# Attention over head pairs: narrow and wide query tiles by turns, alternating memory for queries and keys, and a second ring of score banks

## The chip, the cores and the metric

The kernel runs on one core of a Trainium2 chip. A core has a matrix engine (TensorE, PE in the profile, with its weight loads shown as PEld), a vector engine (VectorE, DVE), a scalar engine for activations (ScalarE, ACT), a general engine (GpSimd, POOL) and a queue engine that issues transfers (SyncE, SP). Each engine runs its own instructions in order, and semaphores order them against each other. Matmuls write into PSUM, here eight banks of 128 partitions by 512 fp32 values; other tiles lie in SBUF; the rest is in the device's main memory and is moved by DMA.

The metric is the device time of the whole kernel in microseconds (us), as the median of several executions. A profile shows one execution.

## The reference

One layer of a hybrid decoder on an input of 1024 positions by 1024 features: a joint projection, then an attention group and an RWKV-7 group of eight heads of 64 each, an output projection and a feed-forward block. What matters here is the attention group:

```
for (window, dilation) in ((128, 1), (512, 4), (2048, 16)):
    query t attends to t, t-d, t-2d, ..., t-window          (causal)
o = sum over the three branches of exp(m - m_all) * acc, divided by the same sum over l
attn = rms_norm(o) * attn_out_gain
mixed = concat([attn, rw]) @ w_out
```

The three branches have the same scores and differ only in which keys they admit. The kernel therefore computes one softmax per head over all causal keys, with a bias that depends on the distance of key and query only: minus infinity where no branch admits the key, and the logarithm of the number of branches otherwise. This bias is the tile `stripT`.

## The kernel before

The whole program is written as straight code through a layer that places tiles in rings of buffers (a pool's `tag` is a ring, `bufs` its length), sets the semaphores, and orders the instructions of ACT, DVE, POOL and SP by a plan of its own, with a priority that `hi_pri` raises. The order on PE is the one in which the code is traced, from line 1055 on by hand (`pe_order`). A tile's first write waits until the last reader of the tile that held its buffer before is done.

Attention handles four pairs of heads (`p`), per pair eight tiles of 128 queries (`i`) and two heads (`h`): 64 steps `m`. Tile `i` has 128 * (i + 1) causal keys, so tile 0 is the narrowest and tile 7 the widest. The parts of a step:

- `at_load(p)` (line 847) brings queries and keys of a pair from main memory through the ring `raw` (two buffers, shared with the values), splits them into a high and a low part on POOL and DVE (`qs`, `kh`, `kl`), and leaves six tiles of 4 KB per partition. The rings `qs`, `kh` and `kl` have two buffers, one per head, so a pair's tiles take the places of the pair before.
- `at_s` (880) computes one tile's scores `pS` on PE in one or two banks (first 512 keys, then the rest), adds the bias and takes the row minimum on DVE (`mn`), and takes the exponential with its sum on ACT. The result is in `Sx`, a ring of three. The banks are of ring w (two banks); the second half goes to ring z (two banks) in pair 1 and in part of pair 2 (line 892).
- `at_t` (900) transposes `Sx` on PE into banks a and c, and copies them to `PT` (ring of six): the first four blocks on ACT, the others on DVE.
- `at_vt` (870) transposes the pair's values, through the same banks a and c, to `Vt` (one buffer).
- `at_v(p, i0)` (914) multiplies two tiles' `PT` by `Vt` into `po`: tiles 0 to 3 in bank b, tiles 4 to 7 in bank y. After every second call it divides by the sums into `ao` (one buffer), stores `ao` to `a_d`, and squares it for the norm (`sqa`, `sq4`).

The main loop (1089) issues in each step the scores of the tile two steps ahead, the transposes of its own tile, and after some steps an `at_v`. Tiles come in the order 0, 1, ... 7, each with head 0 and head 1. `at_load(p + 1)` is traced in a pair's second step. Between the steps lie the last steps of the projection that feeds attention (`rest`, up to step 6), the loads and splits of the output matrix's eight slabs (`load_wo`), and the output projection of the RWKV half for two token tiles (`r_ahead`, 1059: transposes `mxtr` and 24 matmuls `pm` each, in both banks of ring z) from steps 45 and 53 on. A third `r_ahead` stands at the end.

`open_mix` (955), at step 31, gives up the memory of the projection's inputs and opens the pools `tcomb` (attention's half of the output matrix) and `mix` (what the output projection needs). After the loop the norm's factor `sa` is computed on DVE, `half_a` (980) loads and scales the attention output `ma`, transposes it (`mxta`) and the rest of the output projection follows.

Of the kernel before, what the change touches and what calls it, by code (L numbers as in the profile page):

```python
# [17 lines left out]
P = 128  # L18
S = 1024
# [21 lines left out]
def hybrid_kernel(tc, x, par, cst, strip, win, wup_lora, gup, gnwb, grow, wout, wup, wdown, out, dbg=None):  # L41
# [22 lines left out]
    with (  # L64
# [779 lines left out]

        at, sx, pts, pos = {}, {}, {}, {}

        def at_load(p):

            QS, KH, KL = [], [], []
            for h in range(2):  # L850
                qr = ap_.tile([P, S], F32, name=f"qr{p}_{h}", tag="raw")
                for d in range(2):
                    nc.sync.dma_start(qr[own[d]], zs_d[12 + p, h * 64:h * 64 + 64, :])
                qs = ap_.tile([P, S], F32R, name=f"qs{p}_{h}", tag="qs")
                G.tensor_scalar(qs, qr, -0.125, 0.0, op0=OP.mult, op1=OP.add)
                V.scalar_tensor_tensor(qs[64:128], qr[64:128], -0.125, qs[64:128].bitcast(F32), OP.mult, OP.subtract)
                QS.append(qs)
            for h in range(2):
                kr = ap_.tile([P, S], F32, name=f"kr{p}_{h}", tag="raw")
                for d in range(2):  # L860
                    nc.sync.dma_start(kr[own[d]], zs_d[16 + p, h * 64:h * 64 + 64, :])
# [18 lines left out]
        def at_s(p, i, h):  # L880

            QS, KH, KL = at[p]
            w = P * (i + 1)
            if i == 0 and h == 0:
                at[p, "den"] = sm.tile([P, 8, 2], F32, name=f"den{p}", tag="den")
                at[p, "rden"] = sm.tile([P, 8, 2], F32, name=f"rden{p}", tag="rden")
# [27 lines left out]
        def at_v(p, i0):  # L914

            Vt, qg = at[p, "v"], i0 // 4
            if i0 % 4 == 0:
                pos[p, qg] = ps.tile([P, 4, 2, 64], F32, name=f"po{p}_{qg}", tag="by"[qg], bufs=1)
            po = pos[p, qg]
            for i in (i0, i0 + 1):  # L920
                for h in range(2):
                    PT = pts.pop((p, i, h))
                    for j in range(i + 1):
                        mm_h(po[:, i % 4, h], PT[:, j], Vt[:, j, h * 64:h * 64 + 64], j == 0, j == i)
            if i0 % 4 == 0:
                return
            rden = at[p, "rden"][:, 4 * qg:4 * qg + 4]
# [27 lines left out]
        def open_mix():  # L955
# [37 lines left out]
        def mix_x1(t, pm, y=None):  # L993
# [5 lines left out]
            if y is None:  # L999
                y = mp.tile([P, D], F32, name=f"y{t}", tag="y")  # L1000
                src = pm
# [57 lines left out]
        def r_ahead(i, keep):  # L1059
# [11 lines left out]
            if keep:  # L1071
                pms[i] = pm
                return
            part[i] = M["mp"].tile([P, D], F32, name=f"y{ORD[i]}", tag="y")
            for n in range(2):
                A.activation(part[i][:, n * 512:n * 512 + 512], pm[n], AF.Copy)

        ahead = {i: r_ahead(i, i == 2) for i in range(3)}
        LEAD = 28
        for _ in range(LEAD):  # L1080
            next(rest, None)
        hi_pri = lambda: tc.high_priority(offset=PRI[3])
        step = lambda m: (m // 16, m % 16 // 2, m % 2)
        with hi_pri():
            at_load(0)
            at_s(*step(0))
            at_s(*step(1))
            at_vt(0)
        for m in range(64):
            p, i, h = step(m)  # L1090
            with hi_pri():
                if i == 7:
                    at_t(p, i, h)
                    if h == 0:
                        at_v(p, 4)
                    else:
                        if p < 3:
                            at_s(p + 1, 0, 0)
                            at_s(p + 1, 0, 1)
                            at_v(p, 6)  # L1100
                            at_vt(p + 1)
                else:
                    at_s(p, (m % 16 + 2) // 2, h)
                    at_t(p, i, h)
                    if h == 1 and i in (2, 4):
                        at_v(p, i - 2)
                    if h == 1 and i == 0 and p < 3:
                        at_load(p + 1)
# [5 lines left out]
            if m in (13, 21) or m in (29, 37):  # L1114
                k = {13: 4, 21: 5, 29: 6, 37: 7}[m]
                load_wo(k, w2p, "w2")
            if m == 31:
                open_mix()
            if m in (43, 45, 47, 49):
                load_wo((m - 43) // 2, M["tp"], "woA")  # L1120
            for i_, m0 in ((0, 45), (1, 53)):
                if m0 <= m < m0 + 9:
# [8 lines left out]
        for _ in ahead[2]:  # L1131
            pass
        tp, tp_ctx, mp, mix_ctx = M["tp"], M["tc"], M["mp"], M["mc"]
        gpM = mp.tile([P, D], F32, name="gpM", bufs=1)
# [118 lines left out]
        HT = {k: v[1:] for k, v in TS.items()}  # L1253
        mix_ctx.__exit__(None, None, None)
        if "x1" in dbg:
            nc.sync.dma_start(dbg["x1"], x_d)
# [260 lines left out]
```

## Time and profile before

| | |
|---|---|
| median of 3 runs | 1368.56 us (1368.4 to 1368.89) |
| profiled execution | 1369.49 us; its span, first to last instruction, 1367.7 us |
| mean granted TensorE clock | 0.986 |
| bytes moved by DMA | 231.09 MB, 169 GB/s over the span |
| first scores to last `po` matmul | 479.02 to 645.63 us |

Busy times of the engines in the page are sums over the span; an engine that is busy half of the time may still set the end in one stage and have nothing to do in another. Views used further on: the page itself; groups of waits (engine and line that waited, what it waited for, total us, times, longest); the timeline (start and duration in us, engine, line, operation, output and inputs, shapes, count, in brackets the idle time before it and what ended it); busy times by stretch (length, then busy time and count for PE, PEld, DVE, ACT and POOL, then granted clock, DMA share and GB/s); and the chain of work that ended last (start, duration, engine and tile, count).

### The profile page before, as it was taken

Reading aid. Unit: us, or ns where it says so; the run is one execution under the profiler, and the core shown is the slowest. Engines: PE = TensorE matmul, PEld = TensorE weight load, DVE = VectorE, ACT = ScalarE, POOL = GpSimd, SP = SyncE. Lnnn points to the kernel's source line nnn. Section 1 sums busy time; section 2 is a strip of 40 time slices with the busy share of each in tenths; the row PEclk is TensorE's granted clock in tenths of the full one; section 3 lists DMA queues with packets and bytes.
Section 4 is the critical chain, followed back from the end, with each engine's and each line's share of the span. In section 5 each row is a group of like instructions: output and inputs, shape, how many; then the busy total and the mean of one; then the engine's idle time right before and its main releaser. Section 6 shows DMA issues by size and latency. Waiting matters only on the chain.

```text
span 1367.7 us, 23518 instructions
## 1 busy us (share of the span) xinstructions
PE 1291.0 (94%) x9360; PEld 1063.5 (78%) x9360; DVE 914.4 (67%) x1647; ACT 626.3 (46%) x1026; POOL 45.9 (3%) x56
## 2 busy tenths in 40 slices
PE   6999999999999988789998999999999999999997
PEld 5777888788777867678787788888888888888875
DVE  7867757531678576555698986777666776445686
ACT  7652324233455376455556444444343444443442
POOL 0000000000000101010000000000000002000110
PEclk9999999999999999999999999999999999999999
DMA  6346747676584663321333344443456995346554
GB/s 253 114 169 162 193 107 195 184 203 211 169 248 147 200 211 91 86 70 40 123 123 133 137 169 170 153 145 135 161 200 211 327 349 182 92 128 210 187 204 165
DMA packets 161197, 231.09 MB, mean 169 GB/s; under 512 B 51680, under 2 KB 88800, under 8 KB 161088
## 3 DMA queue, kind: packets, MB, share of 16 engines
q1 hardware_dynamic: 153024, 208.62, 47.2%
q10 hardware_dynamic: 8064, 20.98, 4.5%
q8 instruction: 73, 1.20, 0.4%
q14 instruction: 36, 0.29, 0.1%
HBM read 156.66 MB, written 72.89 MB: 168 GB/s over the span
## 4 chain that ended last, share of the span: by engine, by line
PE 74%; DVE 13%; DMA 6%; ACT 4%; issue 2%; SPq 0%; POOL 0%; DVEq 0%; ACTq 0%; POOLq 0%
PE X L47 11%; PE dX L47 8%; PE Z L47 6%; PE pm L47 6%; PE dZ L47 5%; PE z_aq L47 3%; PE dY L47 3%; PE z_av L47 3%; PE po L47 3%; PE z_ak L47 3%; PE Y L47 3%; PE z_v L47 3%; PE z_k L47 3%; PE pT L908 2%; PE pS L47 2%
## 5 line engine op out<-in xcount | busy, mean ns | idle before, releaser
L47 PE MATMUL dX<-wow,wou 128*128 128x512 f32 x768 | 176.2, 390 | 2.3 <-DVE wow L1179 1.6
L47 PEld LDWEIGHTS dX<-wow,wou 128*128 128x128 f32 x768 | 143.8, 188 | 34.1 <-DVE wow L1179 3.4
L47 PE MATMUL dZ<-wow,wou 128*128 128x512 f32 x384 | 87.4, 389 | 0.0
L47 PEld LDWEIGHTS dZ<-wow,wou 128*128 128x128 f32 x384 | 72.1, 188 | 15.0
L1178 ACT ACTIVATE wow<-wd 128x1024 fp32r<-128x1024 f32 x40 | 42.3, 1060 | 88.9 <-PE dZ L47 29.8
L1179 DVE TENSOR_TENSOR wou<-ur,wou 128x1024 fp32r<-128x1024 f32 x56 | 72.0, 1287 | 8.4 <-ACT wou L1178 8.3
L1179 DVE TENSOR_TENSOR wow<-wd,wow 128x1024 fp32r<-128x1024 f32 x40 | 49.9, 1250 | 34.7 <-ACT wow L1178 34.1
L1178 ACT ACTIVATE wou<-ur 128x1024 fp32r<-128x1024 f32 x56 | 58.5, 1048 | 20.9 <-DMA ur<-u_d 13.4
L908 PE MATMUL pT<-cst,S 128*128 128x128 f32 x288 | 47.1, 290 | 18.4 <-DVE PT L912 12.2
L898 ACT ACTIVATE S<-S,mn 128x128 f32<-128x128 f32 (+7 forms) x64 | 49.4, 772 | 19.2 <-DVE mn L896 18.4
L908 PEld LDWEIGHTS pT<-cst,S 128*128 128x128 f32 x288 | 34.4, 146 | 28.7 <-issue 11.1
L1265 ACT ACTIVATE r<-u 128x512 f32<-128x512 f32 x48 | 30.0, 626 | 52.4 <-DVE u L1263 52.0
L896 DVE CUSTOM_DVE_ANT_0 S<-pS,stripT 128x512 f32<-128x512 f32 (+3 forms) x64 | 37.6, 590 | 23.5 <-PE pS L47 18.6
L47 PE MATMUL pm<-WO,mxr 128*128 128x512 f32 x192 | 49.4, 400 | 0.5 <-DVE mxr L972 0.5
L47 PE MATMUL z_aq<-hT,wh_aq 128*128 128x512 f32 x128 | 46.5, 417 | 3.5 <-DVE ev_v L202 3.5
L1179 DVE TENSOR_TENSOR wow<-TK,wow 128x1024 fp32r<-128x1024 f32 x16 | 20.8, 1301 | 38.9 <-ACT wow L1178 38.9
L47 PE MATMUL z_k<-hT,wh_k 128*128 128x512 f32 x128 | 44.9, 412 | 1.7 <-DVE z L233 1.4
L47 PE MATMUL Z<-HB,wo 128*128 128x512 f32 x192 | 46.1, 389 | 0.0
L47 PE MATMUL pm<-WO,mxa 128*128 128x512 f32 x192 | 45.8, 394 | 0.0
L47 PE MATMUL X<-HB,wo 128*128 128x512 f32 x180 | 43.6, 390 | 1.6 <-ACT HB L1034 1.6
L47 PE MATMUL z_av<-hT,wh_av 128*128 128x512 f32 x128 | 44.9, 405 | 0.0
L910 ACT ACTIVATE PT<-pT 128x512 f32<-128x512 f32 (+3 forms) x64 | 32.8, 512 | 26.0 <-PE pT L908 17.2
(388 smaller groups left out, 3097.0 us busy)
## 6 DMA issues: line engine op xcount, KB each, us to landing
ur<-u_d SPq DMA_DIRECT2D x56, 512.0 KB, 4.3
wd<-in_wdown_dram SPq DMA_DIRECT2D x40, 512.0 KB, 4.2
u_d<-S SPq DMA_DIRECT2D x64, 256.0 KB, 2.1
u_d<-u SPq DMA_DIRECT2D x48, 256.0 KB, 2.1
wr_upa<-in_wup_dram SPq DMA_DIRECT2D x16, 512.0 KB, 3.6
wr_upb<-in_wup_dram SPq DMA_DIRECT2D x16, 512.0 KB, 4.0
TK<-in_wdown_dram SPq DMA_DIRECT2D x16, 512.0 KB, 7.3
x<-in_x_dram SPq DMA_DIRECT2D x8, 512.0 KB, 8.1
```

What stands on the lines that cost most here:

```text
L47: return PE.matmul(o, lhsT, rhs, start=start, stop=stop, skip_group_check=True)
L896: V.tensor_tensor_reduce(Sx[:, lo:hi], pS[:, :hi - lo], stripT[:, so:so + hi - lo], 1.0, 3e38 if k == 0 else mn[:, 0:1], OP.add, OP.min, a ...
L898: A.activation(Sx[:, :w], Sx[:, :w], AF.Exp, scale=-1.0, bias=mn[:, nbk - 1:nbk], accum_out=at[p, "den"][:, i, h:h + 1])
L908: PE.transpose(pt[:, j], Sx[:, (4 * k + j) * P:(4 * k + j + 1) * P], ident)
L910: A.activation(PT[:, 0:nb_], pt[:, 0:nb_], AF.Copy)
L1178: A.activation(w[:, 0, 0:n], raw, AF.Copy)
L1179: E.tensor_tensor(w[:, 1, 0:n], raw, w[:, 0, 0:n].bitcast(F32), OP.subtract)
L1265: A.activation(r, src, AF.Relu)
```

## The change

- The tiles of a pair come in the order 0, 4, 1, 5, 2, 6, 3, 7 (`TO`).
- Queries and keys of pairs 1 and 3 go to a pool of their own, `attn1`, with the same six tiles; it lies in the memory that `open_mix` frees, and `open_mix` moves from step 31 to step 7, where pair 1's load is traced too. Pairs 2 and 3 are loaded from steps 17 and 33.
- The second half of a tile's scores uses ring z from pair 1 on, and in pair 0 for tiles 6 and 7.
- `at_v` opens both `po` banks at a pair's start and follows the order `TO`; both are closed by `at_out`, one behind the other, at the pair's end. The last `at_v` of a pair is issued in the second step of the next pair, and `at_vt` behind it.
- Slabs of the output matrix are loaded at other steps (`WOM`), the two `r_ahead` start at steps 38 and 48, the tile `y` gets a pool of its own (`mixy`), and the pool `mix` is opened after the loop, when `attn1` is closed.

```diff
-        at, sx, pts, pos = {}, {}, {}, {}
+        at, sx, pts, pos, aset = {}, {}, {}, {}, {0: ap_}
+        TO = [0,4,1,5,2,6,3,7]
...
-                qs = ap_.tile([P, S], F32R, name=f"qs{p}_{h}", tag="qs")
+                qs = aset[p % 2].tile([P, S], F32R, name=f"qs{p}_{h}", tag=f"qs{h}", bufs=1)
...
-                kh = ap_.tile([P, S], F32R, name=f"kh{p}_{h}", tag="kh")
-                kl = ap_.tile([P, S], F32R, name=f"kl{p}_{h}", tag="kl")
+                kh = aset[p % 2].tile([P, S], F32R, name=f"kh{p}_{h}", tag=f"kh{h}", bufs=1)
+                kl = aset[p % 2].tile([P, S], F32R, name=f"kl{p}_{h}", tag=f"kl{h}", bufs=1)
...
-                pS = ps.tile([P, 512], F32, name=f"pS{p}_{i}_{h}_{k}", tag="wz"[k] if p == 1 or p == 2 and i < 6 else "w")
+                pS = ps.tile([P, 512], F32, name=f"pS{p}_{i}_{h}_{k}", tag="wz"[k] if p > 0 or TO.index(i) > 4 else "w")
...
-            Vt, qg = at[p, "v"], i0 // 4
-            if i0 % 4 == 0:
-                pos[p, qg] = ps.tile([P, 4, 2, 64], F32, name=f"po{p}_{qg}", tag="by"[qg], bufs=1)
-            po = pos[p, qg]
-            for i in (i0, i0 + 1):
+            Vt = at[p, "v"]
+            if i0 == 0:
+                pos[p] = [ps.tile([P, 4, 2, 64], F32, name=f"po{p}_{qg}", tag="by"[qg], bufs=1) for qg in range(2)]
+            for i in TO[i0:i0 + 2]:
                 for h in range(2):
                     PT = pts.pop((p, i, h))
                     for j in range(i + 1):
-                        mm_h(po[:, i % 4, h], PT[:, j], Vt[:, j, h * 64:h * 64 + 64], j == 0, j == i)
-            if i0 % 4 == 0:
-                return
+                        mm_h(pos[p][i // 4][:, i % 4, h], PT[:, j], Vt[:, j, h * 64:h * 64 + 64], j == 0, j == i)
+                if i0 == 6:
+                    at_out(p, i // 4)
+
+        def at_out(p, qg):
+            po = pos[p][qg]
             rden = at[p, "rden"][:, 4 * qg:4 * qg + 4]
...
-            M["mc"] = tc.tile_pool(name="mix", bufs=2)
-            M["mp"] = M["mc"].__enter__()
+            M["yc"] = tc.tile_pool(name="mixy", bufs=2)
+            M["yp"] = M["yc"].__enter__()
+            M["ac"] = tc.tile_pool(name="attn1", bufs=1)
+            aset[1] = M["ac"].__enter__()
...
+        WOM = {17: 4, 19: 5, 33: 6, 35: 7, 37: 0, 49: 1, 51: 2, 53: 3}
...
-        step = lambda m: (m // 16, m % 16 // 2, m % 2)
+        step = lambda m: (m // 16, TO[m % 16 // 2], m % 2)
...
         for m in range(64):
-            p, i, h = step(m)
+            p, h = m // 16, m % 2
+            i = m % 16 // 2
             with hi_pri():
...
+                if m + 2 < 64:
+                    at_s(*step(m + 2))
+                at_t(*step(m))
+                if h == 1 and i % 2 == 0 and m > 1:
+                    at_v(*((p, i - 2) if i else (p - 1, 6)))
+                if h == 1 and i == 0:
+                    at_vt(p)
+                if m == 17 or m == 33:
+                    at_load(p + 1)
...
             if m == 7:
                 for _ in rest:
                     pass
...
+                open_mix()
+                with hi_pri():
+                    at_load(1)
...
-            for i_, m0 in ((0, 45), (1, 53)):
+            for i_, m0 in ((0, 38), (1, 48)):
...
+        M["ac"].__exit__(None, None, None)
+        tp, tp_ctx = M["tp"], M["tc"]
+        mix_ctx = tc.tile_pool(name="mix", bufs=2)
+        mp = M["mp"] = mix_ctx.__enter__()
```

More of the change, by code (lines that the diff above doesn't have):

```diff
@@ L883, in at_s @@
             w = P * (i + 1)
-            if i == 0 and h == 0:
+            if (p, "den") not in at:
                 at[p, "den"] = sm.tile([P, 8, 2], F32, name=f"den{p}", tag="den")
@@ L999, in mix_x1 @@
             if y is None:
-                y = mp.tile([P, D], F32, name=f"y{t}", tag="y")
+                y = M["yp"].tile([P, D], F32, name=f"y{t}", tag="y")
                 src = pm
@@ L1073, in r_ahead @@
                 return
-            part[i] = M["mp"].tile([P, D], F32, name=f"y{ORD[i]}", tag="y")
+            part[i] = M["yp"].tile([P, D], F32, name=f"y{ORD[i]}", tag="y")
             for n in range(2):
@@ L1113, in hybrid_kernel @@
                     pass
[L1114 to L1117, printed above, removed]
                 open_mix()
-            if m in (43, 45, 47, 49):
-                load_wo((m - 43) // 2, M["tp"], "woA")
-            for i_, m0 in ((0, 45), (1, 53)):
+                with hi_pri():
+                    at_load(1)
+            if m in WOM:
+                k = WOM[m]
+                load_wo(k, w2p if k > 3 else M["tp"], "w2" if k > 3 else "woA")
+            for i_, m0 in ((0, 38), (1, 48)):
                 if m0 <= m < m0 + 9:
@@ L1254, in hybrid_kernel @@
         mix_ctx.__exit__(None, None, None)
+        M["yc"].__exit__(None, None, None)
         if "x1" in dbg:
```

19 lines of the change are left out of this document (removed).

## The prediction

> **What bounds the kernel now.** First the page's totals and its chain that ended last.
>
> ```profile
> span 1367.7 us, 23518 instructions
> ...
> PE 1291.0 (94%) x9360; PEld 1063.5 (78%) x9360; DVE 914.4 (67%) x1647; ACT 626.3 (46%) x1026; POOL 45.9 (3%) x56
> ...
> PE 74%; DVE 13%; DMA 6%; ACT 4%; issue 2%; SPq 0%; POOL 0%; DVEq 0%; ACTq 0%; POOLq 0%
> ```
>
> TensorE (PE) bounds the kernel, so the change is worth what it takes out of PE's idle and slow time in the attention loop, the only stage whose work is reordered. The stage runs from the first scores (479.02 us) to the end of the last `po` matmuls (645.63), 166.6 us. I cut it where each head pair's first score matmul starts, with a fifth stretch, the last pair's, where PE hardly waits.
>
> ```profile
> 479.02:517.94 38.92, 32.82 (x315) 26.49 (x314) 29.00 (x68) 27.25 (x57) 5.27 (x4) 0.91 0.67 215
> 517.94:556.76 38.82, 30.88 (x419) 25.88 (x418) 23.76 (x65) 22.75 (x53) 4.68 (x4) 0.96 0.28 76
> 556.76:598.27 41.51, 33.15 (x426) 27.18 (x425) 25.62 (x67) 23.23 (x54) 3.33 (x4) 0.96 0.30 87
> 598.27:645.63 47.36, 44.97 (x593) 39.36 (x591) 23.19 (x66) 27.58 (x59) 0.97 (x1) 0.96 0.12 37
> 607.63:645.63 38.00, 37.14 (x456) 32.08 (x454) 20.08 (x59) 25.22 (x53) 0.00 (x0) 1.00 0.12 36
> ```
>
> After the stretch's length stand busy PE, weight loads, DVE, ACT and POOL, then the granted clock. No engine is full in pairs 1 and 2: PE, DVE and ACT wait for each other. Next, the waits of the stage (total, times, longest) and two stretches of 5 us, one in pair 1's narrow tiles and one in its wide ones.
>
> ```profile
> POOL qs L855 <- PE pS L47: 92.6, 6, 32.6
> POOL kh L132 <- DMA kr<-zs_d: 20.1, 7, 3.8
> PE pT L908 <- DVE PT L912: 12.2, 7, 3.9
> PEld pT L908 <- ACT PT L910: 8.4, 18, 1.2
> PEld pS L47 <- DVE mn L896: 5.3, 10, 1.2
> DVE kl L865 <- POOL kh L132: 5.0, 3, 3.3
> PEld pT L908 <- ACT Vt L878: 3.7, 4, 1.2
> ```
>
> ```profile
> 523.00:528.00 5.00, 3.44 (x19) 1.95 (x17) 2.82 (x10) 4.45 (x14) 0.00 (x0) 1.00 0.62 157
> 538.00:543.00 5.00, 3.49 (x39) 2.97 (x35) 4.12 (x11) 3.35 (x6) 0.00 (x0) 1.00 0.19 56
> ```
>
> Two losses show. In a pair, narrow tiles come first and load ACT (4.45 of 5 us), wide ones last and load DVE (4.12); PE is at 3.5 in both. Between pairs, POOL cannot write the next `qs` before the last score matmul has read the old one (92.6 us of waits). The boundary from pair 1 to pair 2, and rows of the others:
>
> ```profile
> 546.80 3.25 SPq L861 DMA_DIRECT2D kr<-zs_d  x4
> ...
> 547.71 1.22 DVE L856 SCALAR_TENSOR_TENSOR qs<-qr,qs 64x1024 fp32r<-64x1024 f32 x1 [0.21 <-POOL qs L855]
> ...
> 550.34 2.64 PE L908 MATMUL pT<-cst,S 128*128 128x128 f32 x11 [3.85 <-DVE PT L912]
> ...
> 551.50 1.04 POOL L132 TENSOR_SCALAR kh<-kr 128x1024 fp32r<-128x1024 f32 x1 [3.82 <-DMA kr<-zs_d]
> ...
> 559.13 0.33 PE L47 MATMUL pS<-kl,qs 128*128 128x128 f32 x1 [1.84 <-DVE kl L865]
> 559.39 5.26 PE L47 MATMUL po<-Vt,PT 128*64 128x64 f32 x120
> ```
>
> ```profile
> 510.41 2.68 PE L908 MATMUL pT<-cst,S 128*128 128x128 f32 x11 [3.60 <-DVE PT L912]
> 513.02 4.14 PE L47 MATMUL po<-Vt,PT 128*64 128x64 f32 x88
> ...
> 590.97 0.52 PE L908 MATMUL pT<-cst,S 128*128 128x128 f32 x3 [1.26 <-DVE PT L912]
> 593.39 0.66 PE L908 MATMUL pT<-cst,S 128*128 128x128 f32 x4 [1.02 <-DVE PT L912]
> 599.29 0.33 PE L47 MATMUL pS<-kh,qs 128*128 128x128 f32 x1 [0.60 <-POOL kh L132]
> 600.55 0.33 PE L47 MATMUL pS<-kl,qs 128*128 128x128 f32 x1 [0.93 <-DVE kl L865]
> 600.80 5.27 PE L47 MATMUL po<-Vt,PT 128*64 128x64 f32 x120
> ```
>
> DVE's `qs` instructions stand ahead of the score reductions, so transposes wait 3.6 to 3.9 us; then keys are loaded (3.82), split and waited for; and after such gaps matmuls run slower, as the clock row shows:
>
> ```profile
> 508.00:513.00 5.00, 2.59 (x11) 2.07 (x11) 4.97 (x8) 1.24 (x2) 1.04 (x1) 0.62 0.87 228
> ```
>
> **What a pair costs when PE is covered.** Rates, from the chain and from the timeline of PE:
>
> ```profile
> 642.05 3.65 PE po L47 x120
> ...
> 654.02 5.48 PE pm L47 x24
> ```
>
> ```profile
> 606.00 1.09 PE L877 MATMUL vt<-cst,vT 128*128 128x128 f32 x8
> 606.85 0.94 PE L47 MATMUL pm<-WO,mxr 128*128 128x512 f32 x3
> ```
>
> A 512-wide matmul is 5.48/24 = 0.228 us, a `po` matmul 3.65/120 = 0.030, a transpose 0.85/8 = 0.106 (606.00 to 606.85). The stretch 607.63 to 645.63 holds pair 3 without its two first tiles' scores and its eight `vt` transposes, and 44 `pm` matmuls (10.0) and eight `mxtr` transposes (0.85) besides. So a covered pair is 38.0 - 10.85, plus 0.85 for `vt` and 0.5 for the first scores (four narrow matmuls, at most 0.228 each): **28.5 us**. The stage's work is then 4 x 28.5 + 21 leftover projection matmuls (4.8; seven calls of three) + 48 `pm` (10.9) + 12 `mxtr` (1.3) = 131.0, and the excess now 166.6 - 131.0 = **35.6 us**.
>
> Of it at the boundaries: into pair 1, the wait 3.6, eleven transposes in 2.68 instead of 1.2 and 88 `po` in 4.14 instead of 2.7: 6.5. Into pair 2, 3.85 + 1.4 + 1.84 + (5.26 - 3.65) = 8.7. Into pair 3, 1.26 + 1.02 + 0.60 + 0.93 + 1.6 = 5.4. Together **20.6**; the other **15.0** lie inside the pairs.
>
> The Trainium skill (Perfetto Trace Analysis, section Identifying the Most-Contended Engine) says that matmul busy time is no measure of the headroom, and that the busy share of weight loads is. By busy PE the four pairs hold only 24.8 us of idle time, and the best time would be 1345. By weight loads, pair 1's 25.88 at the covered stretch's share (32.08/38.00) would take 30.7 us, a gain of 8.1 where the covered pair gives 10.3. So the trace agrees with the page that busy PE hides part of the loss.
>
> **The change part by part.**
>
> *Memory of their own for pairs 1 and 3.* The loads of pair p+1 are traced where they were, a pair early, but their writes no longer wait for the pair before: the 92.6 us go, and with them the boundaries' 20.6. Added instructions: none; each load still issues 8 query and key DMAs on SP and 4 DVE and 4 POOL instructions, now in the middle of a pair; behind a `kl` that waits for its keys score reductions queue on DVE, and PE waits for those. Now DVE waits for keys 5.0 us in all, 3 times. `attn1` lies where the projection's inputs were, so its first writes wait for the leftover projections, which end in pair 0's first tiles, most of a pair before they are needed. Value: the full 20.6; from below nothing, if the planner issues them late anyway.
>
> *Narrow and wide by turns.* Same instructions. Between a wide tile's scores and its transposes now lie the other head's wide scores, narrow transposes and a `po` block, so small work no longer exposes ACT, and DVE's wide reductions (bounded by 25.62 us of DVE per pair against 28.5 of PE) spread. The waits of transposes on ACT's copies and of scores on DVE's reductions (8.4 + 5.3, some of them in the sum above as drains) should mostly go; those on `Vt` (3.7) stay, since `vt` still shares the transposes' banks. I leave 3.7 + 3.8, a good quarter of 13.7: **7.5 us**. Ends: 0 and all 15.0.
>
> *Second score ring.* The second half of a wide tile goes to z for pair 0's last and all later pairs. z also holds `pm`, now from step 38 on, among pair 2's and 3's scores. Those wait for the copy of `pm` (ACT), which has no high priority; one copy is about a 512-wide ACT instruction, some 0.6 us. Four copies, 0 to 2.4 us; inside the 7.5.
>
> *`po` in two banks, both closed at a pair's end.* Both outputs come one behind the other through one `ao` buffer: the second waits for the first's store.
>
> ```profile
> DMA to landing us min/median/max: 2.2/2.2/4.2
> ...
> 645.75 0.69 DVE L930 TENSOR_TENSOR ao<-po,rden 128x512 f32<-128x512 f32 x1 [2.62 <-PE po L47]
> ...
> 651.38 0.59 PE mxta L969 x4
> ```
>
> Inside the loop the next use of those banks is four steps off; score reductions may queue behind the second `ao` on DVE, bounded by nothing and one landing (4.2) per pair, and I take nothing, since the planner has other reductions to put before it. At the end it does: tile 3's `po` ends 64 matmuls (1.95) before tile 7's, its `ao` takes 0.8, its store 2.2, so the last `ao` starts 3.1 after it instead of 2.0: **+1.1**, not hidden, since `pm` covers only until 651.38 and the next `pm` starts at 654.02. Ends: 0 and 3.0 (landing 4.2).
>
> *Moved.* WO's loads and splits come later in the trace (planner's gap fillers, eight each on ACT and DVE, inside the ends above); `gpM`, `gF` and the first `ma` go behind the last scores or the last stores on SP, all needed later than that. I take nothing; if a load is late, one landing, 4 us. The `Vt` copies move behind the first tiles' scores, nothing.
>
> Sum against the profiled execution's own 1369.49: 35.6 - 7.5 - 1.1 = 27.0, giving 1342.5. That execution lies 0.9 above the runs' median of 1368.56, so **1342**, rounded.
>
> **The rivals.**
>
> *Only the reload goes* (the in-pair 15.0 stay, because two steps of lookahead still expose the chain of reduction, exponential and copy): 20.6 - 1.1 = 19.5, 1349. For it: DVE at 25.6 and ACT at 23.2 per pair leave little slack in order. Against: in the covered stretch PE kept going with the same lookahead.
>
> *Nearly all goes*: 35.6 - 1.1 = 34.5, 1334.
>
> *Slower: DVE is held by transfers.* Loads and paired outputs now stand amid the reductions in DVE's order. If every key landing that POOL now waits for (20.1) held DVE, and each of four pairs' second `ao` waited a store's longest 4.2, 36.9 us would stand against 27.0 saved: 1378. It decides from 27.0 us of such waits, about 7 per pair; against it, DVE was held only 5.0 in all.
>
> *No change:* the planner puts the loads behind `ao`'s stores in SP's order, which already holds SP for long, so that they come as late as now, and the in-pair gain is given back by the same late loads: 1368.
>
> ```profile
> SPq L932 <- DVE ao L930: 63.3, 7, 14.7
> ```
>
> Against it, the loads now come a whole pair early, and a hold of 14.7 us is half a pair.
>
> The Trainium skill (TensorE: Matmul & The Clock Gate, section Why this matters for your kernels) says that PE gaps above about 3 us bring the half clock back. The trace agrees at 3.60 and 3.85, but 5.27 for 120 `po` also followed gaps of 0.60 and 0.93, so shorter ones suffice when crowded. A leftover half-clock window here cost 1.6 us (5.26 - 3.65), within the ends of the in-pair term.
>
> **How the numbers follow.** Forecast (1335 to 1346) 0.52; only the reload goes (1346 to 1355) 0.28; nearly all (below 1335) 0.10; no change 0.03; slower 0.07. The range takes the forecast and its neighbours up to the point where 2 in 10 are left: 1333 to 1353. About 0.2% (2.7 us) is what a measurement of this kernel can tell from no change: faster 0.90, same 0.03, slower 0.07.
>
> **What would show it.** POOL's wait for `pS` under 10 us; no PE wait above 2 us from the first scores to the last `po`; clock 1.00 there; distances between the pairs' first scores near 31 us (37 with a block of `pm`); the stage near 139 us. Wrong if DVE's waits for `kl`, `qs` or the second `ao` grow past a few us, if score matmuls wait for z, or if DVE is busy 9 tenths while PE waits.

## The result, and the profile after

The changed kernel took 1351.68 us (median of 4: 1350.42, 1351.15, 1352.2 and 1360.09) beside 1368.72 for the kernel before: a ratio of 0.9887, with a 95% interval of 0.9846 to 0.9927. It was measured twice more, with ratios of 0.9882 (0.9849 to 0.9914) and 0.9861 (0.9836 to 0.9886); none of those eight executions took more than 1353.46, so 1360.09 is no trait of it. It is faster, by some 17 us where some 27 were forecast. 1351.68 is just inside the range; by the ratio, on the 1368.56 of before, the time is 1353.1, just above it. The profiled execution took 1350.42, 19.1 less than the one before. First the page of the changed kernel, the totals and the chain that ended last.

```profile
span 1348.4 us, 23518 instructions
...
PE 1282.9 (95%) x9360; PEld 1059.3 (79%) x9360; DVE 913.8 (68%) x1647; ACT 625.4 (46%) x1026; POOL 45.6 (3%) x56
...
PE 70%; DVE 15%; DMA 7%; issue 4%; ACT 3%; POOL 0%; SPq 0%; DVEq 0%; ACTq 0%; POOLq 0%
```

The same 23,518 instructions, and the same busy time on DVE, ACT and POOL within a microsecond; only PE's busy time fell, by 8.1. The work is unchanged; what gained is its order and the memory that it uses. Next the busy times by stretch, cut as before at each pair's first score matmul.

```profile
478.69:512.96 34.27, 28.44 (x324) 23.07 (x322) 25.71 (x64) 25.56 (x54) 5.22 (x4) 1.00 0.67 194
512.96:544.22 31.26, 28.55 (x420) 24.69 (x416) 27.06 (x69) 23.02 (x53) 5.56 (x5) 1.00 0.55 153
544.22:583.21 38.99, 35.57 (x445) 30.71 (x442) 24.38 (x68) 24.33 (x56) 3.14 (x3) 0.96 0.27 75
583.21:623.28 40.07, 39.97 (x565) 35.10 (x563) 24.30 (x68) 27.23 (x60) 0.00 (x0) 1.00 0.18 56
```

The stage is 144.6 us long, 22.0 shorter. Length less busy PE summed over the pairs is PE's idle time: 24.8 before, 12.1 now, a gain of 12.7. The other 9.3 is busy PE itself, 141.8 before and 132.5 now: the clock stands at 1.00 in three pairs, where it stood at 0.91 to 0.96 in all. (By this cut a pair's end falls into the next stretch, as it did before; so pair 3 holds 96 `po` matmuls and 16 transposes more than pair 1, beside 28 `pm`.) Pair 3 is covered almost without a gap (0.1 us idle); the idle time is in pairs 0 to 2. From the groups of waits, the stage and the tail behind it:

```profile
...
POOL qs L856 <- PE pS L47: 18.8, 2, 11.0
...
PEld pT L909 <- ACT PT L911: 8.8, 14, 2.2
...
DVE ao L933 <- DMA a_d<-ao: 3.4, 3, 2.3
...
PEld pS L47 <- DVE mn L897: 2.9, 8, 0.9
...
PE pT L909 <- DVE PT L913: 2.4, 3, 1.2
PEld pT L909 <- ACT Vt L879: 2.3, 2, 1.2
...
DVE kl L866 <- POOL kh L132: 0.9, 2, 0.5
```

POOL's wait for the pair before fell from 92.6 to 18.8, and the transposes' wait for DVE's copies from 12.2 to 2.4. What did not move is the transposes' wait for ACT's copies (8.4 before, 8.8 now). The timeline shows what stands ahead of those copies in the two largest gaps of pair 0:

```profile
482.44 1.06 ACT L953 ACTIVATE WO<-wo 128x1024 fp32r<-128x1024 f32 x1 [1.58 <-DMA wo<-in_wout_dram]
483.40 0.81 ACT L899 ACTIVATE S<-S,mn 128x640 f32<-128x640 f32 x1
...
484.21 0.25 ACT L911 ACTIVATE PT<-pT 128x128 f32<-128x128 f32 x1
...
484.52 0.33 PE L909 MATMUL pT<-cst,S 128*128 128x128 f32 x1 [2.06 <-ACT PT L911]
```

```profile
495.21 1.15 ACT L950 ACTIVATE WO<-wo,par 128x1024 fp32r<-128x1024 f32 x1
...
495.86 2.04 DVE L857 SCALAR_TENSOR_TENSOR qs<-qr,qs 64x1024 fp32r<-64x1024 f32 x1
...
497.49 0.66 PE L909 MATMUL pT<-cst,S 128*128 128x128 f32 x4 [1.45 <-ACT PT L911]
```

In the first, ACT holds the split of a slab of the output matrix at the head of its queue, and the slab has not landed: 1.58 us of waiting and 1.06 of splitting pass before the exponential that PE needs. In the second a split on ACT stands ahead, and the `qs` of the next pair on DVE holds the reduction and the `PT` copy behind it (0.84 us more of PE waiting at 498.98). The splits are traced from step 17 on, in pairs 1 to 3, but the planner draws them forward: three stand before the stage on ACT and five in pair 0. It did the same in the kernel before, where ACT's five in pair 0 start at 482.7 to 504.9. So the splits have hardly moved. What moved is pair 1's load: its `qs` on DVE start at 495.9 and 498.9, where they started at 505.6 and 507.8, and they now stand among the splits.

### The profile page after: what moved, and what is told of

It is laid out like the page before. It is cut to its first block, busy times and chain, and to the rows that moved or that the text cites. A ratio compares the mean times of both kernels' runs of the same rounds, so it can differ in the third digit from the quotient of the medians.

```text
span 1348.4 us, 23518 instructions
## 1 busy us (share of the span) xinstructions
PE 1282.9 (95%) x9360; PEld 1059.3 (79%) x9360; DVE 913.8 (68%) x1647; ACT 625.4 (46%) x1026; POOL 45.6 (3%) x56
## 4 chain that ended last, share of the span: by engine, by line
PE 70%; DVE 15%; DMA 7%; issue 4%; ACT 3%; POOL 0%; SPq 0%; DVEq 0%; ACTq 0%; POOLq 0%
PE X L47 12%; PE dX L47 8%; PE Z L47 6%; PE pm L47 6%; PE dZ L47 5%; PE dY L47 3%; PE z_v L47 3%; PE Y L47 3%; PE z_k L47 3%; PE z_aq L47 2%; PE z_ak L47 2%; PE z_r L47 2%; PE qu L47 2%; PE z_av L47 2%; DMA wd<-in_wdown_dram 2%
## 5 line engine op out<-in xcount | busy, mean ns | idle before, releaser
L909 PE MATMUL pT<-cst,S 128*128 128x128 f32 x288 | 44.4, 279 | 9.5 <-ACT PT L911 5.2
L1440 POOL TENSOR_TENSOR E<-E,gpF 128x512 f32<-128x512 f32 x12 | 20.3, 1702 | 721.9 <-DMA xf<-x_d 555.1
```

The source lines that it names most:

```text
L909: PE.transpose(pt[:, j], Sx[:, (4 * k + j) * P:(4 * k + j + 1) * P], ident)
L1440: G.tensor_tensor(e, e, gn[n], OP.mult)
```

## The experiments

Each kernel is the changed one with the edit shown, unless another is named. Times are medians, ratios are against the kernel before on the same chip. A stage length is that of the one profiled execution; the changed kernel's three give 144.6, 142.1 and 142.1.

**The changed kernel again.** No edit.

> The changed kernel once more, nothing edited. If the 1360.09 us among its first four times is a trait of this kernel, one time in four again lies some 9 us above the rest; if it was a disturbance of that moment, all lie at 1350 to 1353.

Measured 1352.2 (1348.48 to 1353.35), and in a later call:

> The changed kernel once more, as the neighbour of the three others on their chip: 1350 to 1354.

1350.9 (1349.56 to 1353.46). The profiles of the same program differ in two places, which make up the 2.5 us between the stage lengths. Pair 0 took 34.27 us and then 33.24 and 33.26, because the wait for the slab's load at the stage's start differs. Pair 2 took 38.99 and then 37.38 and 37.47, because in the first profile alone matmuls ran at half clock behind a gap that all three have (the last section shows it). In the first repeat's timeline:

```profile
481.27 1.06 ACT L953 ACTIVATE WO<-wo 128x1024 fp32r<-128x1024 f32 x1 [0.44 <-DMA wo<-in_wout_dram]
...
483.36 0.33 PE L909 MATMUL pT<-cst,S 128*128 128x128 f32 x1 [0.92 <-ACT PT L911]
```

**Memory without the order.** The second ring and the moved steps stay.

```diff
-        TO = [0,4,1,5,2,6,3,7]
+        TO = list(range(8))
...
-                if i0 == 6:
+                if i in (3, 7):
                     at_out(p, i // 4)
```

> The changed kernel with the tiles in their old order 0 to 7 (pairs 1 and 3 keep their own memory; the first output of a pair is closed after tile 3 again). Theory on record: memory takes the boundaries' 20.6 us and the order 7.5 of the 15.0 inside the pairs, less 1.9 for the tail, so that this kernel is slower than the changed one by 5 to 6 us: about 1356. Rival, memory does it all and the order nothing: 1348 to 1350, no slower than the changed kernel.

1357.3, ratio 0.992 (0.9895 to 0.9945), as the theory on record said (1356), but not for its reasons: 12.6 us gained where the boundaries were to give 20.6. Pair 0 shows why:

```profile
480.68:519.98 39.30, 30.61 (x300) 25.25 (x298) 28.38 (x68) 26.79 (x56) 5.16 (x4) 0.91 0.63 185
```

It took 38.92 before. POOL's wait for the last scores fell from 92.6 us to 12.4, and pair 0's time did not fall. In this profile ACT waits 1.99 us for a late slab and PE stands 3.07 us behind that; PE stands another 2.01 us behind a reduction that a `qs` on DVE holds. It is the slowest of the six executions, so the late slab weighs more in it than in the median.

**The order without the memory.**

```diff
-            M["ac"] = tc.tile_pool(name="attn1", bufs=1)
-            aset[1] = M["ac"].__enter__()
+            aset[1] = ap_
...
-        M["ac"].__exit__(None, None, None)
```

> The changed kernel with all four pairs' queries and keys in the same six tiles (the order of the tiles, the steps of the loads and all else as changed). Theory on record: the boundaries' 20.6 us come back, about 1371, with POOL's qs waiting for pS some 90 us in all. Rival, the order alone covers most of a reload, since a narrow tile's work and a block of po stand beside it: 1356 to 1362.

1373.13, ratio 1.0043 (1.0018 to 1.0068): slower than the kernel before. By themselves the parts are worth +12.6 and -3.2 us, together 17.7: the order gains only where the memory is there. Groups of waits, timeline and busy times by stretch (pair 0) of this run:

```profile
POOL qs L856 <- PE pS L47: 99.5, 6, 35.6
```

```profile
524.15 0.48 PE L47 MATMUL pS<-kh,qs 128*128 128x128 f32 x1 [5.34 <-POOL kh L132]
525.41 0.48 PE L47 MATMUL pS<-kl,qs 128*128 128x128 f32 x1 [0.78 <-DVE kl L866]
```

```profile
479.82:524.15 44.33, 31.30 (x323) 26.24 (x321) 26.68 (x66) 27.22 (x56) 3.13 (x3) 0.85 0.64 191
```

The reload is as long as before the change (99.5 and 92.6), and PE stands 5.34 us at the boundary. The order puts a widest tile's scores last too, so that little may be left to cover the reload; this reason is argued, no run tests it.

**The second ring as before.**

```diff
-                pS = ps.tile([P, 512], F32, name=f"pS{p}_{i}_{h}_{k}", tag="wz"[k] if p > 0 or TO.index(i) > 4 else "w")
+                pS = ps.tile([P, 512], F32, name=f"pS{p}_{i}_{h}_{k}", tag="wz"[k] if p == 1 or p == 2 and TO.index(i) < 6 else "w")
```

> The changed kernel with ring z for the second half of the scores only in pair 1 and in pair 2's first six tiles, as before the change. Theory on record: the ring is worth 0 to 2.4 us and its price (pm shares z) is inside that, so 1349 to 1354. Rival, the ring carries the covered wide tiles: score matmuls wait for a reduction in every wide tile of pairs 0 and 3, 8 tiles at 0.5 to 1 us, 1355 to 1360.

1356.39, ratio 0.9914 (0.9886 to 0.9942), where the changed kernel in the same call has 0.9882. The rival's size, about 4 us, though the intervals overlap; the profiled stage took 151.4. The loss is only in part where the rival put it: the scores' weight loads wait 5.5 us for reductions in the stage, 2.9 in the changed kernel; against the first repeat pair 0 takes 3.7 us more and pair 3 only 0.7, but pair 1, whose ring is the same in both kernels, 4.6. Pair 1's largest gap (2.25 us at 526.8, with half clock after it) is not the ring's: the planner put a second `ao` early there, as in the kernel with one slab below. What the ring is worth by itself stays open.

**The tail.** Two buffers for `ao`; or a last pair whose first output closes early; or both.

```diff
-            ao = ap_.tile([P, 4, 2, 64], F32, name=f"ao{p}_{qg}", tag="ao", bufs=1)
+            ao = ap_.tile([P, 4, 2, 64], F32, name=f"ao{p}_{qg}", tag="ao", bufs=2)
```

> The changed kernel with two buffers for ao. Theory: the tail's extra loss is the second ao's wait for the first one's store (2.30 us) and the half clock that follows, so the time from the last po to the first pm of the other half falls from 10.7 to about 8.4 and the kernel by 2 to 4 us. Rival: the tail is the order's own (a narrow and a wide output end together, so two divisions, two squares and two sums stand one behind the other on DVE and ACT), and this kernel gains under 1 us.

```diff
+        TOP = [TO, TO, TO, [0,4,1,2,5,3,6,7]]
...
-            for i in TO[i0:i0 + 2]:
+            for n_, i in enumerate(TOP[p][i0:i0 + 2]):
...
-                if i0 == 6:
+                seen = TOP[p][:i0 + n_ + 1]
+                if sum(a // 4 == i // 4 for a in seen) == 4 and (p == 3 or i0 == 6):
                     at_out(p, i // 4)
...
```

> The changed kernel with pair 3's tiles in the order 0, 4, 1, 2, 5, 3, 6, 7, its first output closed after tile 3. Theory: the tail is as before the change again (8.1 us from the last po to the next pm, 722 us from the last po to the end), 2.7 to 3.5 us less, and pair 3, which pm covers, loses under 1 us. Rival: with two narrow and two wide tiles side by side pair 3 loses as much as it did with the old order (2 us and more), and nothing is gained.

> The changed kernel with pair 3's order and two buffers for ao alone: the tail 2.5 us shorter, 1347 to 1350.

1349.22 (0.9856), 1350.3 (0.9852) and 1351.56 (0.9853), intervals of about 0.25% to either side. The last `po` to the first `pm` of the attention half takes 8.6, 8.2 and 8.2 us, where the changed kernel's three profiles have 10.8, 10.7 and 10.4 and the kernel before 8.1. The mechanism is as the theory says; the gain in the whole time, some 2 us, is at the edge of what these runs resolve, and the two cures are cures of one wait. The changed kernel's tail, in its timeline and in its chain:

```profile
621.46 0.69 DVE L933 TENSOR_TENSOR ao<-po,rden 128x512 f32<-128x512 f32 x1 [0.18 <-PE po L47]
...
625.84 0.69 DVE L933 TENSOR_TENSOR ao<-po,rden 128x512 f32<-128x512 f32 x1 [2.30 <-DMA a_d<-ao]
...
631.50 0.66 PE L974 MATMUL mxta<-cst,ma 128*128 128x128 f32 x4 [2.55 <-ACT ma L988]
```

```profile
622.18 3.53 DMA a_d<-ao
```

The store took 3.53 us to land, not 2.2. With two buffers the second `ao` follows at once:

```profile
621.59 0.69 DVE L933 TENSOR_TENSOR ao<-po,rden 128x512 f32<-128x512 f32 x1 [0.18 <-PE po L47]
623.58 0.68 DVE L933 TENSOR_TENSOR ao<-po,rden 128x512 f32<-128x512 f32 x1
```

**The splits moved.** To POOL, all eight (a slab scaled, copied to the high part and subtracted there):

```diff
...
-                A.activation(w[:, 0], raw, AF.Copy)
-                V.tensor_tensor(w[:, 1], raw, w[:, 0].bitcast(F32), OP.subtract)
+                G.tensor_scalar(raw, raw, ga, 0.0, op0=OP.mult, op1=OP.add)
+            gcopy(w[:, 0], raw)
+            G.tensor_tensor(w[:, 1], raw, w[:, 0].bitcast(F32), OP.subtract)
```

> The changed kernel with all splits of the output matrix (eight slabs; six fall in pair 0, about 1.1 us on ACT and 1.24 on DVE each) moved to POOL. Theory: what is left inside pairs 0 and 1 is these splits, standing ahead of copies and reductions, so the gaps of 0.9 to 2.1 us near 483, 496 and 515 go and the kernel falls by 3 to 5 us; pair 0 takes about 30 us in place of 33 to 34. Rival: the planner only puts them where ACT and DVE wait anyway, and what is left are the chains of reduction, exponential and copy: under 1 us.

1360.94, ratio 0.9937 (0.9913 to 0.9961): slower than the changed kernel, with 46.8 us in pair 0. The waits name the reason:

```profile
DVE kl L866 <- POOL kh L132: 12.9, 3, 6.4
...
PE pT L909 <- DVE PT L913: 7.8, 1, 7.8
```

POOL copies `kh` behind the splits, `kl` waits for `kh` at the head of DVE's queue, and a `PT` copy stands behind `kl`. Then to later pairs, by taking six raw slabs from the ring of queries and keys and loading them at other steps:

```diff
-            raw = stg.tile([P, D], F32, name=f"wo{k}", tag="wr", bufs=3)
+            if k in (4, 5):
+                raw = stg.tile([P, D], F32, name=f"wo{k}", tag="wr", bufs=3)
+            else:
+                raw = ap_.tile([P, D], F32, name=f"wo{k}", tag="raw")
...
-        WOM = {17: 4, 19: 5, 33: 6, 35: 7, 37: 0, 49: 1, 51: 2, 53: 3}
+        WOM = {17: 4, 19: 5, 21: 6, 23: 7, 37: 0, 40: 1, 43: 2, 46: 3}
```

> The changed kernel with the raw tiles of six of the output matrix's slabs in the ring of queries and keys, so that their splits come after pair 2's loads and not in pair 0. Theory: the splits in pair 0 are what is left there, and pairs 1 to 3 have room for them: pair 0 falls from 33 or 34 us to 30, the kernel by 2 to 4 us. Rival: pair 0 is limited by its own chains and by the loads of pair 1, and the splits only fill what is idle: within 1 us of the changed kernel, pair 0 at 33.

1355.7, ratio 0.9903 (0.9877 to 0.9929), slower than the changed kernel in the same call (0.9861). Pair 0 stays at 33.6 us and pair 1 grows from 31.3 to 37.2. The rival holds for pair 0. Pair 1's growth is not the splits': ACT's two stand at 535.3 and 538.6, and the largest gap, 2.17 us with half clock after it, comes ahead of them, at 524.7, from a second `ao` that the planner put early. Beside memory alone:

> Memory without the order, and the same late splits. Memory alone left pair 0 at 39.3 us, as long as before, although its boundary should have given 6.5. Theory: the splits and a wait for their load in pair 0 took that back (gaps of 3.07 and 2.01 us), so this kernel is 4 to 6 us faster than memory alone (1357.3): 1351 to 1353. Rival: the moved loads' qs and kl on DVE took it back, and this kernel stays at 1356 to 1358.

1356.47, ratio 0.9895 (0.9873 to 0.9916) against 0.992: some 3 us by the ratios, under 1 by the medians. Pair 0 by itself falls as the theory said:

```profile
480.58:514.90 34.32, 29.11 (x299) 24.19 (x297) 22.57 (x63) 22.35 (x50) 5.74 (x5) 0.95 0.53 152
```

5.0 us less than with memory alone; pair 1 gave 0.9 back. Of the theory's two gaps only the 3.07 behind the late slab is gone. The other stays (2.02 at 495.8): it stands behind the `qs` on DVE, as the rival says. So splits and loads both took from memory's gain. How much each took stays open, with one profile of each kernel and a late slab in one of them.

**The copy of the ahead tile at high priority.**

```diff
-            rx[i] = half_r(ORD[i], "z")
+            with hi_pri():
+                rx[i] = half_r(ORD[i], "z")
```

> The changed kernel with the transposed RWKV tile's copy and its low part (mxr) at the attention loop's high priority. Theory: the 1.52 us gap before the first ahead pm and the half-clock stretch behind it go, 2 to 3 us. Rival: the copies then stand ahead of score reductions, and as much is lost there: within 1 us.

1355.01, ratio 0.989 (0.9867 to 0.9913): no gain. The gap before the first `pm` only fell from 1.52 to 1.19, and this plan met the late slab at its worst, so the run doesn't tell the theories apart:

```profile
483.05 1.06 ACT L953 ACTIVATE WO<-wo 128x1024 fp32r<-128x1024 f32 x1 [4.63 <-DMA wo<-in_wout_dram]
...
484.54 0.33 PE L909 MATMUL pT<-cst,S 128*128 128x128 f32 x1 [3.94 <-ACT S L899]
```

**Tail and late splits together.**

> The three together: pair 3 in the order that ends its first output early, two buffers for ao, and the late splits. If each keeps its gain: 1343 to 1347. If the late splits fill room that the other two need in pair 3: 1349 and more.

1348.58, ratio 0.9841 (0.9817 to 0.9866): the lowest median of the kernels that leave nothing out, below the changed kernel's 0.9861 in the same call, but with overlapping intervals, so no version is shown to beat it. The gains did not add up. Pair 1, with the same late splits but two buffers for `ao`, takes 32.1 us instead of 37.2. Pair 2 takes 41.4: scores wait for a bank of ring z, whose `pm` is copied by ACT (to `y`) behind two splits of 1.14 us each:

```profile
578.45 0.50 PE L47 MATMUL pS<-kh,qs 128*128 128x512 f32 x1 [2.48 <-ACT y L1086]
```

This is the cost that the prediction named for the second ring, 0 to 2.4 us for four copies.

**The loads off DVE.** For pairs 1 to 3 the low parts of queries and keys are made on POOL (load_pool).

```diff
+                if p:
+                    G.tensor_scalar(qr[64:128], qr[64:128], -0.125, 0.0, op0=OP.mult, op1=OP.add)
+                    G.tensor_tensor(qs[64:128], qr[64:128], qs[64:128].bitcast(F32), OP.subtract)
...
-                V.tensor_tensor(kl, kr, kh.bitcast(F32), OP.subtract)
+                (G if p else V).tensor_tensor(kl, kr, kh.bitcast(F32), OP.subtract)
```

> The changed kernel with the low parts of queries and keys (qs' second half, kl) of pairs 1 to 3 made on POOL in place of DVE, 12 instructions of 1.2 to 2.05 us less on DVE. Theory: they are what holds reductions and PT copies in pairs 0 to 2 now that the loads stand in the middle of a pair; the gaps at 495 to 498, 505 and 563 go, 3 to 5 us. Rival: POOL's work slows DVE's beside it (a qs on DVE took 2.05 in place of 1.22 while POOL wrote), and the next pair's keys come later: 0 or slower.

1364.66, ratio 0.9954 (0.9937 to 0.9972): most of the change's gain is lost. Waits and timeline of this run:

```profile
DVE ao L937 <- DMA a_d<-ao: 13.4, 4, 7.4
```

```profile
565.25 0.44 SPq L866 DMA_DIRECT2D kr<-zs_d  x1
565.73 0.59 SPq L939 DMA_DIRECT2D a_d<-ao  x1
...
569.65 0.69 DVE L937 TENSOR_TENSOR ao<-po,rden 128x512 f32<-128x512 f32 x1 [7.38 <-DMA a_d<-ao]
...
571.03 0.45 PE L913 MATMUL pT<-cst,S 128*128 128x128 f32 x1 [6.74 <-DVE PT L917]
```

The first `ao` was ready at 559.6, but its store stands in SP's order behind a load whose `raw` buffer POOL, slower now, frees late. The store is issued at 565.73, the second `ao` waits for it on DVE, and a `PT` copy waits behind that. Pair 0 lost time too (40.3 us), first behind a late slab: ACT waited 3.11 us for it, and PE 3.59. With the tail's two cures the wait is gone:

> load_pool together with pair 3's order that ends the first output early and two buffers for ao. If the parts add up: 1342 to 1347. If the loads on POOL give nothing: 1348 to 1350.

1351.29, ratio 0.9844 (0.9815 to 0.9872), level with the cures alone (0.9853). PE's idle time in pairs 1 and 2 fell from 8.3 to 5.9, in pair 0 it rose from 4.4 to 6.6: there the splits left on DVE took 2.5 us each (median of four) beside POOL's work, not 1.28.

> The same with the late splits of six slabs, into pairs whose DVE is now freer by 5 us each. If DVE's long instructions are what is left: 1340 to 1346, below best. If the splits cost as much wherever they stand: as best or slower.

1358.7, ratio 0.99 (0.9872 to 0.9928). Pair 0, now without splits and without the loads' DVE part, ran in 29.4 us; pair 1 took 42.4. From this run's (best_wo's) timeline:

```profile
541.50 1.06 ACT L962 ACTIVATE WO<-wo 128x1024 fp32r<-128x1024 f32 x1 [6.33 <-DMA wo<-in_wout_dram]
...
543.10 1.11 PE L914 MATMUL pT<-cst,S 128*128 128x128 f32 x4 [6.43 <-ACT PT L916]
```

Again a split that ACT reached before its slab had landed; the whole 6.33 us came through to PE.

**Taken away, not moved.** One slab, split before the stage, stands for all eight.

```diff
         def load_wo(k, pool, tag):
+            if k != 4:
+                WO[k] = WO[4]
+                return
```

> The changed kernel with one slab of the output matrix, split before the stage, standing for all eight: the loads and splits of seven slabs are left out. Theory: the splits, and ACT's waits for their loads, are the part of the residual that the forecast took as nothing; pair 0 falls from 33 or 34 us to about 30 and the kernel by 3 to 5 us, to 1346 to 1349. Rival: the loads' qs and kl on DVE hold pair 0 by themselves, under 1 us.

1349.67, ratio 0.9839 (0.9816 to 0.9861); stage 144.1. By the ratios that is some 3 to 7 us faster than the changed kernel, as the theory wanted, though the intervals overlap. The profile has less than the theory wanted: pair 0 takes 32.0 us, where `qs` and `kl` on DVE still stand ahead of reductions and copies (PE gaps of 1.29 and 0.92 us at 498.0 and 506.1). And pair 1 takes 34.7 us instead of 31.3, for another reason:

```profile
523.34 0.63 ACT L938 ACTIVATE sqa<-ao 128x512 f32<-128x512 f32 x1 [1.34 <-DVE ao L933]
...
524.99 1.33 PE L909 MATMUL pT<-cst,S 128*128 128x128 f32 x5 [1.94 <-ACT PT L911]
```

The second `ao` waits for the first one's store, ACT waits at the head of its queue to square it, and an exponential and a `PT` copy stand behind that; half clock follows. The planner put it so in this kernel, in the one with ring z as before (1.64 us of ACT's waiting) and in the one with late splits (1.57). In the changed kernel's pair 1 ACT does not wait for `ao`.

> The same without seven slabs' loads and splits, and with the low parts of pairs 1 to 3 on POOL, pair 3's order that ends its first output early, and two buffers for ao. If splits, loads and the tail are the whole of what the forecast missed: the stage at 138 to 140 us, the kernel 6 to 9 us below wo_one's neighbour, 1339 to 1344. If chains of reduction, exponential and copy hold the rest: the stage at 142 us and more, the kernel above 1345.

1339.5, ratio 0.9776 (0.9748 to 0.9804). Its stretches, pair by pair:

```profile
476.06:505.50 29.44, 27.77 (x324) 23.09 (x322) 16.41 (x55) 21.20 (x49) 12.73 (x9) 1.00 0.43 120
505.50:537.25 31.75, 28.29 (x421) 24.80 (x417) 20.31 (x62) 22.87 (x53) 18.73 (x12) 1.00 0.42 117
537.25:573.64 36.39, 33.87 (x445) 29.48 (x442) 21.26 (x64) 24.08 (x55) 15.83 (x10) 1.00 0.35 95
573.64:614.91 41.27, 40.29 (x565) 35.17 (x563) 24.12 (x68) 26.59 (x60) 0.00 (x0) 1.00 0.21 66
```

A stage of 138.9 us at full clock. Stage lengths of single profiles can't be compared to a microsecond or two, since the early `ao` and half clock come and go with the plan and the execution. Pair 0 has no `ao` to close, and there the comparison is cleaner:

| pair 0, us | loads' low parts on DVE | on POOL |
|---|---|---|
| splits in pair 0 | 33.2 to 34.3 (six profiles: changed kernel and its tail cures) | 34.5 (with the cures), 40.3 (without, behind a late slab) |
| splits not in pair 0 | 33.6, 33.6 (late), 32.0 (left out) | 29.4 (late), 29.4 (left out) |

Both 33.6, and one of the six (34.0), hold a stretch at half clock (mean clock 0.95); the others stand at 1.00, but for the 40.3 at 0.92. Either taken away alone gives at most 2.3 us in pair 0, both together 3.8 to 4.9: while one class of long instructions is left, it stands ahead of the same copies and reductions. With a split its slab's load is gone from pair 0 too, and the two were not separated.

## Why the prediction was right and wrong

- **Direction, and the reload as its main source: right.** Without memory of their own the gain turns to a loss of 3.2 us. That the boundaries' 20.6 us belong to the memory by itself is wrong: memory alone gave 12.6, and in its profile pair 0 gained nothing, with a split behind a late slab and a `qs` ahead of what PE needed. The rival *only the reload goes* had the time (1349) nearer than the forecast, but not the mechanism: by the medians the order is worth another 5 us on top (the intervals overlap).
- **The in-pair residual of 7.5 us: the chains were sized well, what stands ahead of them was not.** The changed kernel's stage exceeds the 131.0 of work by 13.6 us in the profiled run and by 11.1 in the other two. With the splits and the loads' DVE part gone it exceeds it by 138.9 - 131.0 = 7.9; that this is so near 7.5 is partly luck, as it is one profile and the 7.5 was a share of waits chosen by judgement. So the step that failed is *Moved*, "planner's gap fillers ... I take nothing", with the memory part's load instructions in the middle of a pair counted at no cost: together they cost 3.2 to 5.7 us in the stage as a whole, and 3.8 to 4.9 in pair 0. The prediction took it that the fillers moved; they stood in pair 0 before, and the load was moved in among them. It named no work that hides them: a filler of 1.06 to 1.28 us, or one that waits for its slab, isn't hidden when exponentials and copies with a waiting PE stand behind it in the same queue. How the sum divides between splits and loads stays open, as in pair 0 neither gives much without the other.
- **The second `ao` inside the loop, taken as nothing: right for the changed kernel, by its plan.** There the planner did put other reductions first, as the prediction said. In three other kernels it did not, and PE stood 1.94 to 2.25 us in pair 1 with half clock behind it. With two buffers for `ao` and the same late splits pair 1 fell from 37.2 to 32.1 us; with two buffers alone it took 34.8, so they are no sure cure of pair 1.
- **The second ring: mis-sized.** Taken as nothing or a small cost; undoing it costs about 4 us by the medians, some of it by the early `ao` in pair 1 and not by the ring.
- **The tail of +1.1: right mechanism, too small.** From the last `po` to the end 722.1 us became 725.1 (725.8 and 724.1 in the repeats), +2 to +4. The store was put at its median landing, 2.2, and took 3.53. A half-clock stretch follows at 634.1; with two buffers for `ao` alone one follows too (at 632.5), so it isn't shown to be the wait's. The upper end given, 3.0, holds the profiled run.
- **The slower rival: not here, but real.** In the changed kernel's stage DVE waited 0.9 us for `kh` (1.2 and 1.0 in the repeats), and 3.4 for `ao`'s store, of which 2.3 fall in the tail. It came as soon as POOL was loaded: 12.9 us behind `kh` with the splits on POOL, 13.4 behind the store in load_pool, with one PE gap of 7.8 and one of 6.74. The margin against it was small.
- **The sum.** 27.0 us were forecast, 19.1 came in the profiled runs: 6.1 are missing in the stage (13.6 - 7.5) and 1.9 in the tail (3.0 - 1.1). Of the 6.1, pair 0 explains 4.8 (34.27 less the 29.44 without splits and loads on DVE) and the half clock of this one execution in pair 2 another 1.5.
- **The signs given.** Stage near 139: 144.6 (142.1 in the repeats), and 138.9 once the fillers are gone. Pair 1's distance near 31: 31.3 (the weight-load estimate that the prediction drew from the Trainium skill, Perfetto Trace Analysis, section Identifying the Most-Contended Engine, was 30.7; the trace agrees, but for this pair busy PE gave 38.82 - 7.9 = 30.9, so it does not tell the two measures apart). POOL's wait under 10: 18.8, which cost nothing, as no score matmul of the stage waited for queries or keys. No PE wait over 2 us: one of 2.06 (0.92 and 1.17 there in the repeats). Clock 1.00: in three pairs of four, in all four in the repeats.

## What to carry to other kernels

When a change closes the large waits, look at what the planner puts into the gaps that are left: a long off-path instruction, and above all one whose load may be late, belongs where nothing urgent stands behind it in its engine's queue. Price moved work by what stands behind it, not by its duration or its engine's busy share. Two edits of which one pays only beside the other (here the order, beside the early loads) should be judged together, and a cost suspected of two things must be tested with both taken away. Before a kernel is compared with its neighbour by single profiles, profile the same program again: here that alone moved the stage by 2.5 us.

## What the runs showed of the hardware

DVE and POOL slow each other. In load_pool's timeline the split on DVE that takes 1.28 us alone took 2.87 beside POOL's subtractions. POOL's `kl` took 3.23 beside another split (from 511.16, 1.30 us), against 2.34 in best_wo, where no split stands beside it:

```profile
502.75 5.72 POOL L859 TENSOR_TENSOR qs<-qr,qs 64x1024 fp32r<-64x1024 f32 x2
...
506.69 2.87 DVE L955 SCALAR_TENSOR_TENSOR WO<-wo,par,WO 128x1024 fp32r<-128x1024 f32 x1
...
511.47 3.23 POOL L870 TENSOR_TENSOR kl<-kr,kh 128x1024 fp32r<-128x1024 f32 x1
```

The Trainium skill (SBUF — State Buffer, section Who interferes with whom) says that a DVE instruction with two inputs in SBUF contends with a POOL instruction that reads SBUF; the trace agrees, both being of that kind.

A gap of PE may bring the half clock or not, for one and the same program and gap. The changed kernel's three profiles have the same gap between the first `pm` matmuls, 1.52, 1.51 and 1.52 us. Behind it the granted clock was 0.66 over 5 us in the first profile and 1.00 in both repeats. Here are the first profile, behind the 2.06 us at 484.5 (no half clock) and behind the 1.52 us, and the first repeat, behind the 1.51 us:

```profile
484.00:489.00 5.00, 4.48 (x31) 4.02 (x32) 3.02 (x11) 4.03 (x12) 0.00 (x0) 1.00 0.74 234
...
564.51:569.51 5.00, 5.00 (x18) 4.21 (x19) 1.87 (x5) 1.61 (x3) 0.00 (x0) 0.66 0.00 1
```

```profile
563.39:568.39 5.00, 5.00 (x64) 4.28 (x66) 2.65 (x8) 2.34 (x5) 0.00 (x0) 1.00 0.00 0
```

Two kernels with the loads off DVE show the same for a longer gap: 3.67 us at 511.6 in load_pool was followed by 0.66, and 3.67 us at 510.1 with the tail's cures by 1.00. So the length of the gap alone doesn't decide, and the 3 us named in the prediction are no bound in either direction here. What decides was not tried.
